# The scan's operand products, the fill's low parts and the scaling of attention's output, from POOL to VectorE

## The chip, the cores and the metric

The kernel runs on one core of a Trainium2 chip. Its time is device microseconds of one execution. TensorE (PE) multiplies matrices; VectorE (DVE), ScalarE (ACT) and GpSimd (POOL) do elementwise work; SyncE (SP) issues most of the DMA transfers. Each engine takes its own queue of instructions in order, and waits on semaphores for what the others have to deliver.

## The reference

One layer of an encoder for 1024 prompt and 256 sample tokens (1280 columns in all), width 1024. Two branches read the same modulated input `h @ w_in`: latent attention with 8 heads, and a recurrence with 8 heads of 64 channels, run once forward and once backward over the tokens. Their outputs are gated, added and projected, and a feed-forward part follows. The part of the recurrence that matters here, for each head and direction:

```python
def step(S, inp):
    r_t, w_t, k_t, v_t, kk_t, a_t = inp
    sa = einsum('bhvk,bhk->bhv', S, -kk_t)
    S = S * w_t + sa[..., :, None] * (kk_t * a_t)[..., None, :] + v_t[..., :, None] * k_t[..., None, :]
    y = einsum('bhvk,bhk->bhv', S, r_t)
    return S, y
```

and beside it `o_mla = softmax(q k) v @ w_mla_o`, and the gates `sigmoid(h @ w_in[gate columns])`.

## The kernel before, in words

Stages follow each other: input products of the recurrence, input products of attention with seven of the sixteen gate tiles, attention, then **the scan with the fill beside it**, then merge, output product, norm and the feed-forward part. Matrix products in the large stages split each factor into a rounded high part and a low part (`hi`, `lo`) and add three products. A weight tile comes by DMA (`wraw`), ScalarE rounds it to `whi`, and another engine subtracts to `wlo` (line 55): POOL unless the caller names VectorE.

The scan (`phase_rwkv`) goes over ten batches of 128 tokens, each in both directions, each in two steps of 64 tokens. For one batch:

- `front` (line 763 on) loads the batch's decay sums, keys and so on, runs a prefix sum on VectorE (`L`, line 774), centres it (line 780), takes exponentials on ScalarE (`E2`, `M`) and multiplies the keys by them into `bk` (line 789: two products 128x512 per direction).
- `left` (line 798 on) makes `lt`: a negated product of `kk` (line 807) and a product of `r` (line 811), four and four of 64x256 per direction and batch.
- `part` multiplies `lt` with `bk` on PE; ScalarE copies the results out, POOL masks them (lines 733 and 738). Of them come the 16 small triangular matrices `aa`.
- `invert` inverts these on VectorE: a transpose `X` (line 856), 31 times a multiply and an addition (lines 865 and 867, the tiles `xt` and `W`), two transposes (869, 871), then two groups of small products on PE (lines 877 and 882, `pw`) with copies between (878, 879, 884, 885).
- `begin` and `step` carry the state `S` through the batch's two steps: products on PE into `py` and `pS`, copied or added by VectorE (`ru` line 917, `xv` line 921, `S` lines 900 and 926) and ScalarE (`yt`, lines 934 and 935). `begin` multiplies two small vectors to `f` (line 895).

The fill (`phase_fill`) is work of other branches that PE does beside the scan: nine gate tiles over three groups of columns (line 1041 the products, line 1154 the tanh), then attention's output: `scaled` loads the unscaled output and the row sums' reciprocals, multiplies them (line 1172), rounds the result on ScalarE (line 1023) and subtracts for the low part (line 1024); `mla_out` multiplies with `w_mla_o` and applies the gate (line 1181). It makes 1368 products of 128x256 or 128x512 on PE. Each gate tile's `whi` and `wlo` are made once, stored, and loaded again for the other two groups of columns. Parts of the merge (`branch`, lines 1063 to 1087) for 512 middle tokens stand near the scan's end too.

The order in each engine's queue is set by a scheduler before the run: it lists the instructions by priority and by a modelled time. The scan's steps have the highest priority (an offset of 4000), the inversions a small one (100), the fill comes after in the program and is put where the model sees room. Tiles have a fixed number of buffers: `ld` (the scan's loads) 5, `bk` 2, `lt` 5 per direction, weights 2, rows of the fill 4, one set for the inversion.

Of the kernel before, what the change touches and what calls it, by code (L numbers as in the profile page):

```python
# [9 lines left out]
ALU = mybir.AluOpType  # L10
# [8 lines left out]
KT = D // P  # L19
# [695 lines left out]
def phase_rwkv(g, ctx):  # L715
# [46 lines left out]
    def front(o, eng):  # L762


        d = o.d

        def cv(ap):
            return ap.rearrange("p (c i) -> p c i", i=64)

        s = load(o, f"s{d}")  # L770
        kq = load(o, f"ka{d}", f"kd{d}"), load(o, f"kd{d}", f"ka{d}")
        kk, r = load(o, "kk"), load(o, "r")
        L, M = half("L"), half("M", 520).rearrange("p (a c i) -> p a c i", a=4, c=2)
        nc.vector.tensor_tensor_scan(L, rst, s, 0.0, ALU.mult, ALU.add)
        f = o.f
        mk = rf.tile([P, 4, 2], F32, tag="mid", name="mid", bufs=2)
        L4 = L.rearrange("p (a c i) -> p a c i", a=4, c=2)
        nc.vector.tensor_scalar(mk, L4[:, :, :, 63], 0.5, None, ALU.mult)
        nc.vector.tensor_scalar(M[:, :, :, 0], mk, -1.0, None, ALU.mult)
        eng.tensor_tensor(M[:, :, :, 1:], L4, mk.unsqueeze(3).broadcast_to([P, 4, 2, 64]), ALU.subtract)  # L780
        E2 = half("E2")
        nc.scalar.activation(E2.rearrange("p (a c i) -> p a c i", a=4, c=2), M[:, :, :, 1:], AF.Exp, scale=-K2)
        nc.scalar.activation(M, M, AF.Exp, scale=K2)
        nc.vector.tensor_tensor(f[:, :, 0:1], mk[:, :, 0:1], mk[:, :, 1:2], ALU.add)
        nc.vector.tensor_copy(f[:, :, 1:3], mk[:, :, ::-1])
        nc.scalar.activation(f, f, AF.Exp, scale=K2)
        bk = rf.tile([P, 8, 2, 64], F32, tag="bk", name="bk", bufs=BK)
        for i in range(2):
            nc.gpsimd.tensor_tensor(bk[:, :, i, :], cv(kq[i]), cv(E2), ALU.mult)
        o.bk, o.kk, o.r, o.L = bk, kk, r, M  # L790

    def values(o):
# [6 lines left out]
    def left(o, st, eng):  # L799
        def pick(ap, rows):  # L800
            return ap[rows].rearrange("p (a c i) -> p a c i", a=4, i=64)[:, :, st, :]
        before, here = o.L[:, :, st, 0:64], o.L[:, :, st, 1:65]
        lt = o.lt[st] = rf.tile([P, 4, 2, P], F32, tag=f"lt{o.d}", name="lt", bufs=LT)
        for e in range(2):
            l = lt[HV[e], :, e, 0:64]
            if eng is nc.vector:
                eng.scalar_tensor_tensor(l, pick(o.kk, HV[e]), -1.0, before[HV[e]], ALU.mult, ALU.mult)
            else:
                eng.tensor_tensor(l, pick(o.kk, HV[e]), before[HV[e]], ALU.mult)
                eng.tensor_scalar(l, l, -1.0, None, ALU.mult)  # L810
            nc.gpsimd.tensor_tensor(lt[HV[e], :, e, 64:128][:, :, ::1 - 2 * o.d], pick(o.r, HV[e]), here[HV[e]], ALU.mult)

    def part(o, st, aa):

# [72 lines left out]
    def begin(bt, sv):  # L887

        if sv.f is None:
            nc.gpsimd.memset(S, 0.0)  # L890
            for e in range(2):
                nc.gpsimd.memset(bt.xv[0][HV[e], :, e, :], 0.0)
        else:
            f = rk.tile([P, 8, 1], F32, tag="fb", name="fb", bufs=2)
            nc.gpsimd.tensor_tensor(f, sv.f, bt.f[:, :, 2:3], ALU.mult)
            place(bt.xv[0], f)

    def place(xv, f):
# [128 lines left out]
def weights(g, src, kt, eng=None):  # L1027
    return [split_w(g, src[:, k0:k0 + 4, :], 4, eng, pool=g.fl, tag=g.ft, rbufs=RB, bufs=WB) for k0 in range(0, kt, 4)]


def product(g, src, kt, parts, ws=None, eng=None):

    ws = ws or weights(g, src, kt, eng)
    for part in parts:
        p = g.fp.tile([P, 512], F32, tag="mm", name="fp")
        c = 0
        for a, n in part:
            for k in range(kt):
                wh, wl = ws[k // 4]
                for i, (ww, aa) in enumerate(((wh, a[0]), (wh, a[1]), (wl, a[0]))):  # L1040
                    g.nc.tensor.matmul(p[:, c:c + n], lhsT=ww[:, k % 4, :], rhs=aa[:, k, :n],  # L1041
                                       start=(k == 0 and i == 0), stop=(k == kt - 1 and i == 2))
            c += n
        yield p[:, :c]
# [73 lines left out]
def phase_fill(g):  # L1118
# [17 lines left out]
    def kept(j, made):  # L1136

        if made is not None:
            for h, w in enumerate(made):
                for e in range(2):  # L1140
                    nc.sync.dma_start(out=g.scr["gw"][j - NB, h, e].bitcast(F32), in_=w[e].bitcast(F32))
            return made
        ws = []
        for h in range(2):
            ws.append([fl.tile([P, 4, P], F32R, tag=g.ft + t, name="w" + t, bufs=WB) for t in ("hi", "lo")])
            for e in range(2):
                nc.sync.dma_start(out=ws[h][e].bitcast(F32), in_=g.scr["gw"][j - NB, h, e].bitcast(F32))
        return ws

    def gate(j, *parts, ws=None):  # L1150
        for p in product(g, io["w_in"][20 + j], KT, [[x[:2] for x in parts]], ws):
            n, c0 = p.shape[-1], parts[0][2]
            t = row("gt", n)
            nc.scalar.activation(t, p, AF.Tanh, scale=0.5)
            nc.sync.dma_start(out=g.scr["gate"][j, :, c0:c0 + n], in_=t)
# [3 lines left out]
    xs = [load(i, c0) for i, c0 in enumerate(spans[0])]  # L1159
    for s in range(3):  # L1160
        for j in js:
            gate(j, *xs, ws=kept(j, weights(g, io["w_in"][20 + j], KT) if s == 0 else None))
        xs = [load(i, c0) for i, c0 in enumerate(spans[s + 1])] if s < 2 else []

    def scaled(a, c0, n):
        for j in range(4):
            raw, bc = row("raw", n), row("bc", n)
            nc.sync.dma_start(out=raw, in_=g.scr["om"][j, :, c0:c0 + n])
            for e in range(2):
                nc.sync.dma_start(out=bc[HV[e]], in_=g.scr["rs"][2 * j + e].rearrange("a t -> (a t)")[c0:c0 + n].unsqueeze(0)  # L1170
                                  .broadcast_to([64, n]))
            nc.gpsimd.tensor_tensor(raw, raw, bc, ALU.mult)
            split_in(g, raw, a[0][:, j, :], a[1][:, j, :])

    def mla_out(*parts):
        for dt in range(KT):
            ts = [row("gt", n) for _, _, n in parts]
            for t, (_, c0, n) in zip(ts, parts):
                nc.sync.dma_start(out=t, in_=g.scr["gate"][dt, :, c0:c0 + n])
            for p, t, (_, c0, n) in zip(product(g, io["w_mla_o"][dt], 4, [[(a, n)] for a, _, n in parts]), ts, parts):  # L1180
                nc.vector.scalar_tensor_tensor(t, t, 1.0, p, ALU.add, ALU.mult)
                nc.sync.dma_start(out=g.scr["xm"][dt, :, c0:c0 + n], in_=t)

# [278 lines left out]
```

## Time and profile before

| | us |
|---|---|
| median of 3 runs (lowest to highest) | 2679.28 (2678.97 to 2682.38) |
| profiled execution | 2674.54 |
| its span | 2672.8 |
| busy in the span: PE / VectorE / ScalarE / POOL | 2498.4 / 1439.4 / 999.9 / 645.9 |
| mean granted TensorE clock | 0.959 of 2.4 GHz |

The span is from the first to the last instruction. Busy time is when an engine works on at least one instruction. PE's busy time comes from modelled ends of pipelined products, so a PE that is busy all the time isn't at its peak. The scan with the fill lies at 885.6 to 1503.3 us of the span, a quarter of it. Stretches are given in microseconds from the span's start.

### The profile page before, as it was taken

The numbers are of one execution on the slowest core, as the hardware profiler recorded it, in microseconds if no ns is written. First come the engines' busy times: TensorE is split into PE (matmuls) and PEld (weight loads), VectorE is DVE, ScalarE is ACT, GpSimd is POOL, SyncE is SP. The second block draws the span as 40 slices with busy tenths as digits, with TensorE's granted clock in tenths as the row PEclk, the third lists the DMA queues.
The fourth block names the chain that finished last, engine by engine and source line by source line (L and its number), as shares of the span: only waits on it lengthen the run. The fifth ranks groups of instructions, "written<-read, shape, count | busy, mean of one in ns | idle before, by whom it ended". The sixth has DMA issues, their size and how long they took to land. (4 is left out here: it accounts for less than half of the span.)

```text
span 2672.8 us, 42383 instructions
## 1 busy us (share of the span) xinstructions
PE 2498.4 (93%) x17018; PEld 2121.9 (79%) x17018; DVE 1439.4 (54%) x2513; ACT 999.9 (37%) x1867; POOL 645.9 (24%) x675
## 2 busy tenths in 40 slices
PE   5999999989998799899997999999999999999997
PEld 3777777778887688888885767788888888888886
DVE  5655652347777678887676587542122222222228
ACT  4422332347676666565552233331110111101114
POOL 2112131021015545443333000132111111111123
PEclk8999999999999688898997999999999999999998
DMA  7654532110003544644655665221111111111113
GB/s 288 230 198 177 211 126 85 47 32 19 18 13 89 173 150 145 196 147 121 191 182 188 203 207 166 89 79 48 40 40 34 38 40 40 40 32 40 40 43 131
DMA packets 188469, 292.36 MB, mean 109 GB/s; under 512 B 16160, under 2 KB 106096, under 8 KB 188272
## 3 DMA queue, kind: packets, MB, share of 16 engines
q1 hardware_dynamic: 174880, 242.07, 28.4%
q0 software_dynamic: 5760, 26.22, 2.4%
q10 hardware_dynamic: 7632, 21.37, 2.3%
q8 instruction: 134, 2.20, 0.3%
q14 instruction: 63, 0.52, 0.1%
HBM read 211.95 MB, written 77.64 MB: 108 GB/s over the span
## 5 line engine op out<-in xcount | busy, mean ns | idle before, releaser
L55 POOL TENSOR_TENSOR wlo<-wraw,whi 128x1024 fp32r<-128x1024 f32 (+2 forms) x149 | 293.9, 1975 | 1343.3 <-ACT whi L53 1129.8
L53 ACT CAST whi<-wraw 128x1024 fp32r<-128x1024 f32 (+2 forms) x212 | 172.6, 819 | 905.3 <-issue 476.1
L67 PE MATMUL mm<-h2h,whi 128*128 128x512 f32 (+1 forms) x1056 | 279.5, 357 | 2.4 <-ACT whi L53 2.4
L67 PE MATMUL mm<-h2h,wlo 128*128 128x512 f32 (+1 forms) x1056 | 279.0, 357 | 1.5 <-POOL wlo L55 1.5
L67 PE MATMUL mm<-h2l,whi 128*128 128x512 f32 (+1 forms) x1056 | 278.5, 356 | 0.0
L67 PE MATMUL mm<-g,whi 128*128 128x512 f32 (+1 forms) x1056 | 240.9, 359 | 6.2 <-DVE ft L1251 5.6
L1041 PE MATMUL fp<-x,whi 128*128 128x256 f32 (+1 forms) x912 | 206.9, 320 | 27.5 <-ACT x L1023 18.4
L67 PEld LDWEIGHTS mm<-g,whi 128*128 128x128 f32 x1056 | 178.0, 190 | 38.0 <-issue 5.7
L67 PEld LDWEIGHTS mm<-h2h,whi 128*128 128x128 f32 x1056 | 177.0, 188 | 33.6 <-ACT whi L53 2.5
L67 PEld LDWEIGHTS mm<-h2h,wlo 128*128 128x128 f32 x1056 | 176.9, 188 | 33.4 <-POOL wlo L55 2.8
L67 PEld LDWEIGHTS mm<-h2l,whi 128*128 128x128 f32 x1056 | 177.1, 188 | 31.2 <-issue 0.5
L1263 DVE SCALAR_TENSOR_TENSOR x<-mm,g2h,x 128x512 f32<-128x512 f32 (+1 forms) x144 | 87.1, 655 | 196.3 <-PE mm L67 196.0
L1041 PEld LDWEIGHTS fp<-x,whi 128*128 128x128 f32 x912 | 156.3, 204 | 39.1 <-ACT x L1023 21.5
L1251 DVE SCALAR_TENSOR_TENSOR ft<-ft,mm 128x512 f32<-128x512 f32 (+1 forms) x66 | 36.1, 594 | 224.2 <-ACT ft L1250 224.1
L67 PE MATMUL mm<-hl,whi 128*128 128x512 f32 (+1 forms) x480 | 147.6, 364 | 7.7 <-DVE hl L265 7.7
L67 PE MATMUL mm<-hh,whi 128*128 128x512 f32 (+1 forms) x480 | 148.0, 366 | 6.4 <-ACT pp L320 3.8
L1041 PE MATMUL fp<-x,wlo 128*128 128x256 f32 (+1 forms) x456 | 146.6, 322 | 6.6 <-POOL wlo L55 3.9
L1252 DVE TENSOR_TENSOR ft<-ft,mm 128x512 f32<-128x512 f32 (+1 forms) x66 | 36.0, 593 | 216.2 <-PE mm L67 216.2
L67 PE MATMUL mm<-hh,wlo 128*128 128x512 f32 (+1 forms) x480 | 145.8, 363 | 0.0
L67 PE MATMUL mm<-g,wlo 128*128 128x512 f32 (+1 forms) x528 | 136.5, 359 | 1.2 <-POOL wlo L55 1.2
L865 DVE TENSOR_TENSOR xt<-W,X 128x126 f32<-128x126 f32 (+22 forms) x310 | 125.8, 406 | 9.0
L867 DVE TENSOR_TENSOR W<-W,xt 128x126 f32<-128x126 f32 (+22 forms) x310 | 120.4, 388 | 8.6
(318 smaller groups left out, 5149.8 us busy)
## 6 DMA issues: line engine op xcount, KB each, us to landing
wraw<-in_w_ffn_in_dram SPq DMA_DIRECT2D x56, 512.0 KB, 3.5
araw<-in_w_ada_dram ACTq DMA_DIRECT2D x32, 512.0 KB, 3.3
wraw<-in_w_ffn_out_dram SPq DMA_DIRECT2D x26, 512.0 KB, 3.6
wraw<-in_w_in_dram SPq DMA_DIRECT2D x20, 512.0 KB, 4.0
x<-scr_h SPq DMA_DIRECT2D x20, 512.0 KB, 7.5
whi<-scr_gw SPq DMA_DIRECT2D x36, 256.0 KB, 3.0
wlo<-scr_gw SPq DMA_DIRECT2D x36, 256.0 KB, 3.5
araw<-in_w_ada_dram SPq DMA_DIRECT2D x16, 512.0 KB, 10.1
```

The lines of the kernel that those rows point to most:

```text
L53: nc.scalar.copy(hi, raw)
L55: (eng or nc.gpsimd).tensor_tensor(lo, raw, hi, ALU.subtract)
L67: nc.tensor.matmul(p[:, :n], lhsT=ww[:, k, :], rhs=aa[:, k, c0:c0 + n], start=(k == 0 and i == 0), stop=(k == kt - 1 and i == 2))
L865: nc.vector.tensor_tensor(tv, W[:, h:, j:j + 1].broadcast_to([P, n, j]), X[:, j:j + 1, 0:j].broadcast_to([P, n, j]), ALU.mult)
L867: nc.vector.tensor_tensor(W[:, h:, 0:j], W[:, h:, 0:j], tv, ALU.add)
L1041: g.nc.tensor.matmul(p[:, c:c + n], lhsT=ww[:, k % 4, :], rhs=aa[:, k, :n], start=(k == 0 and i == 0), stop=(k == kt - 1 and i == 2))
L1251: nc.vector.scalar_tensor_tensor(t[:, :n], t[:, :n], 1.0, u[:, :n], ALU.add, ALU.mult)
L1252: nc.vector.tensor_tensor(t[:, :n], t[:, :n], z[:, :n], ALU.mult)
L1263: nc.vector.scalar_tensor_tensor(x1[:, dt, c0:c0 + n], p[:, :n], g.g2h[:, dt, c0 // TP:c0 // TP + 1], x1[:, dt, c0:c0 + n], ALU.mult, ALU.add)
```

## The change

Seven calls are given to VectorE that were on POOL: the products of `bk` and `lt` in all batches but the first (whose `eng` is POOL, since it is prepared during attention), the product of `f`, the low parts of the fill's weights (gates and `w_mla_o`), and the scaling of attention's output. By the queues 36 of 40 products of `bk`, 72 of 80 of `lt`, all 8 of `f`, 34 low parts and all 12 scalings move.

```diff
--- before.py
+++ after.py
@@ -786,7 +786,7 @@
         nc.scalar.activation(f, f, AF.Exp, scale=K2)
         bk = rf.tile([P, 8, 2, 64], F32, tag="bk", name="bk", bufs=BK)
         for i in range(2):
-            nc.gpsimd.tensor_tensor(bk[:, :, i, :], cv(kq[i]), cv(E2), ALU.mult)
+            eng.tensor_tensor(bk[:, :, i, :], cv(kq[i]), cv(E2), ALU.mult)
         o.bk, o.kk, o.r, o.L = bk, kk, r, M
 
     def values(o):
@@ -808,7 +808,7 @@
             else:
                 eng.tensor_tensor(l, pick(o.kk, HV[e]), before[HV[e]], ALU.mult)
                 eng.tensor_scalar(l, l, -1.0, None, ALU.mult)
-            nc.gpsimd.tensor_tensor(lt[HV[e], :, e, 64:128][:, :, ::1 - 2 * o.d], pick(o.r, HV[e]), here[HV[e]], ALU.mult)
+            eng.tensor_tensor(lt[HV[e], :, e, 64:128][:, :, ::1 - 2 * o.d], pick(o.r, HV[e]), here[HV[e]], ALU.mult)
 
     def part(o, st, aa):
 
@@ -892,7 +892,7 @@
                 nc.gpsimd.memset(bt.xv[0][HV[e], :, e, :], 0.0)
         else:
             f = rk.tile([P, 8, 1], F32, tag="fb", name="fb", bufs=2)
-            nc.gpsimd.tensor_tensor(f, sv.f, bt.f[:, :, 2:3], ALU.mult)
+            nc.vector.tensor_tensor(f, sv.f, bt.f[:, :, 2:3], ALU.mult)
             place(bt.xv[0], f)
 
     def place(xv, f):
@@ -1159,7 +1159,7 @@
     xs = [load(i, c0) for i, c0 in enumerate(spans[0])]
     for s in range(3):
         for j in js:
-            gate(j, *xs, ws=kept(j, weights(g, io["w_in"][20 + j], KT) if s == 0 else None))
+            gate(j, *xs, ws=kept(j, weights(g, io["w_in"][20 + j], KT, nc.vector) if s == 0 else None))
         xs = [load(i, c0) for i, c0 in enumerate(spans[s + 1])] if s < 2 else []
 
     def scaled(a, c0, n):
@@ -1169,7 +1169,7 @@
             for e in range(2):
                 nc.sync.dma_start(out=bc[HV[e]], in_=g.scr["rs"][2 * j + e].rearrange("a t -> (a t)")[c0:c0 + n].unsqueeze(0)
                                   .broadcast_to([64, n]))
-            nc.gpsimd.tensor_tensor(raw, raw, bc, ALU.mult)
+            nc.vector.tensor_tensor(raw, raw, bc, ALU.mult)
             split_in(g, raw, a[0][:, j, :], a[1][:, j, :])
 
     def mla_out(*parts):
@@ -1177,7 +1177,7 @@
             ts = [row("gt", n) for _, _, n in parts]
             for t, (_, c0, n) in zip(ts, parts):
                 nc.sync.dma_start(out=t, in_=g.scr["gate"][dt, :, c0:c0 + n])
-            for p, t, (_, c0, n) in zip(product(g, io["w_mla_o"][dt], 4, [[(a, n)] for a, _, n in parts]), ts, parts):
+            for p, t, (_, c0, n) in zip(product(g, io["w_mla_o"][dt], 4, [[(a, n)] for a, _, n in parts], eng=nc.vector), ts, parts):
                 nc.vector.scalar_tensor_tensor(t, t, 1.0, p, ALU.add, ALU.mult)
                 nc.sync.dma_start(out=g.scr["xm"][dt, :, c0:c0 + n], in_=t)
 
```

The scheduler then orders all queues of this stage anew. Three places show it.

VectorE in the sixth inversion (`xt` and `W` are the inversion's own), before:

```order
L865 TENSOR_TENSOR xt<-W,X 128x126
L867 TENSOR_TENSOR W<-W,xt 128x9x14
L865 TENSOR_TENSOR xt<-W,X 128x130
L867 TENSOR_TENSOR W<-W,xt 128x10x13
L865 TENSOR_TENSOR xt<-W,X 128x120
L867 TENSOR_TENSOR W<-W,xt 128x10x12
L807 SCALAR_TENSOR_TENSOR lt<-ld,M 64x4x64 x2
L917 COPY ru<-py 64x512
L865 TENSOR_TENSOR xt<-W,X 128x121
L867 TENSOR_TENSOR W<-W,xt 128x11x11
L865 TENSOR_TENSOR xt<-W,X 128x110
```

and of the change:

```order
L865 TENSOR_TENSOR xt<-W,X 128x126
L867 TENSOR_TENSOR W<-W,xt 128x9x14
L807 SCALAR_TENSOR_TENSOR lt<-ld,M 64x4x64
L811 TENSOR_TENSOR lt<-ld,M 64x4x64
L807 SCALAR_TENSOR_TENSOR lt<-ld,M 64x4x64
L917 COPY ru<-py 64x512
L811 TENSOR_TENSOR lt<-ld,M 64x4x64
L865 TENSOR_TENSOR xt<-W,X 128x130
L789 TENSOR_TENSOR bk<-ld,E_11399 128x8x64
L867 TENSOR_TENSOR W<-W,xt 128x10x13
L789 TENSOR_TENSOR bk<-ld,E_11399 128x8x64
L865 TENSOR_TENSOR xt<-W,X 128x120
```

The products of `lt` (line 811) and of `bk` (line 789) stand between two steps of the inversion, the former behind the negated product of the same tile, the latter on either side of one step.

VectorE at the end of the eighth inversion, up to the first transpose of the ninth, before:

```order
L865 TENSOR_TENSOR xt<-W,X 128x30
L867 TENSOR_TENSOR W<-W,xt 128x15x2
L865 TENSOR_TENSOR xt<-W,X 128x16
L867 TENSOR_TENSOR W<-W,xt 128x16
L869 STREAM_TRANSPOSE dt<-W 128x32x16
L871 STREAM_TRANSPOSE xr<-dt 128x512
L879 COPY aa<-pw 32x16x32
L856 STREAM_TRANSPOSE X<-aa 128x1024
```

and of the change (`raw` and `x` are attention's output, `gt` its gate):

```order
L867 TENSOR_TENSOR W<-W,xt 128x16
L869 STREAM_TRANSPOSE dt<-W 128x32x16
L1024 TENSOR_TENSOR x<-raw,x 128x256
L871 STREAM_TRANSPOSE xr<-dt 128x512
L1172 TENSOR_TENSOR raw<-raw,bc 128x256 x2
L1024 TENSOR_TENSOR x<-raw,x 128x256 x2
L1181 SCALAR_TENSOR_TENSOR gt<-gt,fp 128x512
L879 COPY aa<-pw 32x16x32
L1181 SCALAR_TENSOR_TENSOR gt<-gt,fp 128x256
L55 TENSOR_TENSOR wlo<-wraw,whi 128x512
L1181 SCALAR_TENSOR_TENSOR gt<-gt,fp 128x512
L856 STREAM_TRANSPOSE X<-aa 128x1024
```

The scaling, the splitting and the gating of attention's output now stand among the last instructions of an inversion, two inversions before the last.

PE from the second half of the scan's last step (`py`, line 931) on, before:

```order
L1041 MATMUL fp<-x,whi 128x512 x2
L1041 MATMUL fp<-x,wlo 128x512
L931 MATMUL py<-xv,arb 64x64 x16
L1041 MATMUL fp<-x,whi 128x256 x2
L1041 MATMUL fp<-x,wlo 128x256
L1041 MATMUL fp<-x,whi 128x256 x2
L1041 MATMUL fp<-x,wlo 128x256
L1041 MATMUL fp<-x,whi 128x256 x2
L1041 MATMUL fp<-x,wlo 128x256
L1041 MATMUL fp<-x,whi 128x256 x2
L1041 MATMUL fp<-x,wlo 128x256
```

and of the change (`or` is the merged output's operand, the next stage's):

```order
L919 MATMUL py<-ru,tt_7623 64x64 x8
L925 MATMUL pS<-xv,bkt 64x64 x8
L931 MATMUL py<-xv,arb 64x64 x8
L913 MATMUL py<-xv,lt 64x64 x32
L919 MATMUL py<-ru,tt_7623 64x64 x16
L931 MATMUL py<-xv,arb 64x64 x16
L1041 MATMUL fp<-or,whi 128x512 x2
L1041 MATMUL fp<-or,wlo 128x512
L1041 MATMUL fp<-or,whi 128x512 x2
L1041 MATMUL fp<-or,wlo 128x512
L1041 MATMUL fp<-or,whi 128x512 x2
```

Before, 20 rows like these last eight, 60 products of the fill, follow the scan's last product; now the next stage's products follow it directly, and 192 instead of 80 of the fill's products stand ahead of the first step.

## Rows read from the trace of the kernel before

**Rows 1.** Busy time by stretch: PE, PEld, VectorE, ScalarE, POOL (count); clock, DMA share, GB/s.

```profile
...
938.60:1000.40 61.80, 58.29 (x685) 53.78 (x686) 47.49 (x98) 35.63 (x79) 31.73 (x43) 0.89 0.50 155
...
1335.90:1379.60 43.70, 42.60 (x619) 39.62 (x620) 32.26 (x80) 29.95 (x68) 14.17 (x26) 1.00 0.54 172
1379.60:1464.40 84.80, 61.85 (x598) 48.89 (x599) 65.07 (x134) 27.14 (x47) 26.32 (x22) 0.83 0.63 194
1464.40:1503.30 38.90, 38.90 (x368) 34.03 (x367) 9.69 (x17) 8.26 (x14) 6.39 (x5) 0.93 0.49 155
...
sum 871.40, PE 786.20 PEld 689.34 DVE 640.69 ACT 422.76 POOL 275.89; mean PE 65.52 PEld 57.44 DVE 53.39 ACT 35.23 POOL 22.99
```

**Rows 2.** Line 856, each inversion's first instruction: ns min/median/max, first and last start.

```profile
L856 DVE STREAM_TRANSPOSE X<-aa x10: 1978/2042/2057, 885.6 to 1379.6; 128x1024 f32<-128x1024 f32 x10
```

**Rows 3.** VectorE's waits, 938.6 to 1379.6: us, times, longest.

```profile
DVE aa L879 <- ACT aa L878: 46.8, 8, 7.5
DVE X L856 <- PE pw L882: 31.2, 9, 5.2
```

**Rows 4.** VectorE in order of time: start, length, instruction.

```profile
1184.77 0.29 DVE L867 TENSOR_TENSOR W<-W,xt 128x126 f32<-128x126 f32 x1
1185.10 1.28 DVE L865 TENSOR_TENSOR xt<-W,X 128x120 f32<-128x120 f32 x1
1186.31 0.67 DVE L926 TENSOR_TENSOR S<-S,pS 128x512 f32<-128x512 f32 x1
1186.90 0.80 DVE L867 TENSOR_TENSOR W<-W,xt 128x120 f32<-128x120 f32 x1
1187.63 0.68 DVE L900 TENSOR_TENSOR S<-S,f 128x512 f32<-128x512 f32 x1
```

**Rows 5.** POOL in the same stretch.

```profile
1184.78 2.78 POOL L789 TENSOR_TENSOR bk<-ld,E 128x512 f32<-128x512 f32 x2 [6.23 <-PE py L931]
```

**Rows 6.** Busy VectorE of the inversion's 62 multiplies and additions, by stretch.

```profile
938.60:1000.40 61.80, 28.45 (x62) 0.89 0.50 155
1335.90:1379.60 43.70, 19.82 (x62) 1.00 0.54 172
```

**Rows 7.** POOL's groups, 885.6 to 1503.3: busy us, mean ns, idle before and releasers.

```profile
L811 POOL TENSOR_TENSOR lt<-ld,M 64x256 f32<-64x256 f32 x68 | 50.2, 738 | 35.2 <-DMA ld<-scr_r 14.4 <-ACT whi L53 12.1 <-DVE W L867 3.0
L789 POOL TENSOR_TENSOR bk<-ld,E 128x512 f32<-128x512 f32 x34 | 45.1, 1340 | 49.1 <-PE py L931 12.5 <-DMA ld<-scr_kd 12.1 <-DMA ld<-scr_ka 10.2
L55 POOL TENSOR_TENSOR wlo<-wraw,whi 128x512 fp32r<-128x512 f32 x33 | 42.2, 1288 | 86.3 <-ACT whi L53 82.9 <-issue 3.1
...
L1172 POOL TENSOR_TENSOR raw<-raw,bc 128x512 f32<-128x512 f32 x8 | 11.4, 1421 | 21.8 <-DMA bc<-scr_rs 16.1 <-DVE xt L865 2.9 <-DVE W L867 2.8
```

**Rows 8.** Line 807, the negated products on VectorE: ns min/median/max.

```profile
L807 DVE SCALAR_TENSOR_TENSOR lt<-ld,M x68: 383/534/2371, 894.7 to 1346.6; 64x256 f32<-64x256 f32 x68
```

**Rows 9.** The chain of waits around the scan's end: start, length, what.

```profile
1502.76 0.59 ACT yt L935
...
1515.48 0.60 DVE wlo L55
```

**Rows 10.** POOL's waits, 938.6 to 1379.6: us, times, longest.

```profile
POOL lt L811 <- DMA ld<-scr_r: 14.4, 5, 4.5
POOL bk L789 <- PE py L931: 12.5, 2, 6.2
POOL bk L789 <- DMA ld<-scr_kd: 12.1, 3, 6.5
POOL bk L789 <- DMA ld<-scr_ka: 10.2, 4, 3.4
```

**Rows 11.** PE's largest group, 1379.6 to 1503.3.

```profile
L1041 PE MATMUL fp<-x,whi 128*128 128x512 f32 (+1 forms) x162 | 51.0, 394 | 20.7 <-ACT x L1023 18.4 <-ACT whi L53 1.2 <-DVE x L1024 1.1
```

**Rows 12.** PE in order of time, from the fill to the next stage.

```profile
1512.42 0.28 PE L1041 MATMUL fp<-x,wlo 128*128 128x256 f32 x1
1513.86 0.73 PE L1041 MATMUL fp<-or,whi 128*128 128x512 f32 x2 [1.16 <-ACT or L1023]
```

## The prediction

> **What bounds the kernel now.** I read the table of stretches first. From 885.6 to 1503.3 us the scan and the fill run side by side, and the windows are cut at the starts of the ten inversions (the reader sees how many, and the first and the last start, in [rows 2]). In [rows 1] the reader is to see that no engine is full there and two are close: over the whole table PE is busy 786 of 871 us, and in the stretch 938.6 to 1000.4 VectorE 47.5 of 61.8 with PE at 58.3. A batch takes 54.9 us on average ((1379.6 - 885.6) / 9 from [rows 2]).
>
> Next the waits of VectorE [rows 3]. Over the eight batches from 938.6 to 1379.6 its two large waits are both inside the inversion: for the copies behind the two small products on PE, 46.8 and 31.2 us, or 9.75 us a batch. The rest of a batch VectorE is at work, with gaps of some 0.04 us between dependent instructions [rows 4]. The inversions stand one behind the other, so a batch lasts as long as VectorE's work in it plus that 9.75. That is the bound of the scan: VectorE's queue, in its order. PE is idle for 3.5 us of the batch from 938.6 [rows 1]: the fill's products take up what the scan leaves.
>
> Then the timeline, VectorE against POOL. [rows 4, 5]: while POOL runs the two products of `bk` (from 1184.78, 2.78 us), an inversion's multiply takes 1.28 us and the next 0.80, where the one before took 0.29. The addition that reads PSUM took 0.67 in the middle of it, as always. POOL's two took 2.78 us there, near twice their mean of 1.34 [rows 7], so they are hardly lengthened. So a part of VectorE's busy time is waiting for POOL. How much, in [rows 6] with the POOL column of [rows 1]: the same 62 instructions took 28.45 us in a batch with 31.73 us of POOL, and 19.82 in one with 14.17. That is 0.49 us of VectorE for 1 us of POOL, for the inversion alone.
>
> **The change part by part.** Everything moved is two-input work of POOL beside the scan [rows 7]: the products of `lt` 50.2 us, of `bk` 45.1, the low parts of the fill 42.2, the scaling 11.4 in eight instructions and, at half of their 1.42 us each, 2.8 in the four of half width: together 152 us. (The eight products of `f`, 128x8, I leave out here and put in below at 1 us in all.)
>
> What goes: 152 x 0.49 = 74 us of stalls in the inversions. The negated products of `lt` on VectorE (68 of them) have a shortest of 0.383 and a median of 0.534 us [rows 8]; 68 x 0.15 = 10 us, of which the moved part of POOL's time (152 of the 276 us in the POOL column's sum) gives some 6. Removed: 80 us.
>
> What comes: by the order 36 products of `bk`, 72 of `lt`, 34 low parts and 12 scalings go to VectorE. VectorE's price of a 128x512 two-input instruction is 0.60 us behind a neighbour [rows 9] to 0.68 alone [rows 4]; of a 64x256 one 0.38 to 0.53 [rows 8], the upper end holding stalls that I expect to go. Low end: 36 x 0.60 + 72 x 0.38 + 34 x 0.60 + 8 x 0.60 + 4 x 0.38 + 1 = 77 us. High end: 24.5 + 38.2 + 23.1 + 5.4 + 2.1 + 1 = 94. I take 80: between two dependent steps of the inversion an independent instruction overlaps its neighbour's end ([rows 4]: 0.67 long, the next starts 0.59 later). So the exchange is even: 0, with ends at -2 and +15, and below, if each us of POOL held VectorE for a whole us, at 77 - 152 = -75.
>
> New waits: VectorE takes its queue in order, and a product that is not ready now holds up the inversion behind it, and the step's copies that PE's next products wait for. On POOL these instructions waited for loads and for the buffer [rows 10]: 14.4 + 12.5 + 12.1 + 10.2 = 49 us in eight batches. POOL came early and had nothing else to do; VectorE comes to them later, since its queue is fuller. Ends: 0 and 49; I take an eighth, +6.
>
> The scaling: POOL took 1.42 us for a 128x512 product [rows 7] and ScalarE, then PE, waited for it; PE's products waited 18.4 us for the rounded `x` in the stretch from 1379.6 [rows 11]. With 0.68 in the place of 1.42, 8 x 0.74 = 6 us of that chain go; I take -5. Ends: -18 and, if the loads behind it set the pace, 0.
>
> The order: PE's queue now ends the fill before the scan ends. Before, 60 of the fill's 1368 products stand behind the last step. The last copy of the scan starts at 1502.76 [rows 9], the fill's last product at 1512.42, and the first of the next stage at 1513.86 [rows 12]: 1513.86 - 1503.35 = 10.5 us. Those products go into PE's idle time from 1379.6 to 1464.4, where PE was busy 61.85 of 84.8 us [rows 1], and what is late next there is the last inversion. Behind the scan the new queue has the next stage's products at once. I take -11. The cost if that cover is gone: the chain of attention's output now stands in the eighth and ninth inversions; [rows 1] show what that mixture does in the tenth, 84.8 us against 54.9. It is not a new cost as long as the tenth gives back what they take.
>
> Sum: 0 + 6 - 5 - 11 = -10 us. The profiled execution took 2674.54 us (span 2672.8), the median of the runs is 4.7 us above it, so 2679.3 - 10 = 2669.
>
> **A rule beside the rows.** On [rows 4, 5]: the Trainium skill, SBUF — State Buffer, section "Who interferes with whom", says that a VectorE instruction with two inputs in SBUF contends with a GpSimd instruction that reads SBUF, and that one with at most one such input does not. The trace agrees: 1.28 against 0.29 us, and 0.67 for the PSUM one. By its exclusive lock for the whole instruction every us of POOL could cost VectorE a us, and the sum would be nearer to the end of -75 than to 0; the measured slope is 0.49.
>
> **The rivals.**
>
> *The waits of the loads move onto VectorE (slower).* Place: VectorE's queue at the products of `bk` and `lt`, in each batch. For it: loads landed just as POOL wanted them [rows 10], and the inversion is the pacer. Against it: VectorE's own two large waits are not for loads [rows 3], and the new queue has inversion steps ahead of each `bk`. Price: two thirds of the 49 us instead of an eighth, +33 for +6, so 2669 + 27 = 2696. It decides from 16 us of such waits: there the gain is gone.
>
> *PE takes the room (no change).* In the batches where the new queue puts more fill ahead of the scan (192 products stand before the first step, 80 before the change) PE has little slack: 58.29 of 61.8 us are busy from 938.6, and 42.60 of 43.7 from 1335.9 [rows 1]. Then the scan ends some 10 us later, and the 11 us behind it only pay for that: 2679. Against it: PE's total work does not change and it has 85 us idle over the table. On the even exchange the Trainium skill speaks too: Perfetto Trace Analysis, section "Optimizing Scalar/DVE Operations", says that since the two engines share a read port, moving work between them might not help; this case's rows agree so far (80 out, 80 in).
>
> *More is given back than the inversions show.* VectorE's other instructions with two SBUF inputs are stalled too. With 0.75 for 0.49, 152 x 0.75 = 114 us go in the inversions' place of 74, which is -40 more and 2629, and PE's 85 us of idle time allow that. For it: a median of 0.534 against a shortest of 0.383 us [rows 8]. Against it: an instruction that reads PSUM, as the 0.67 one in [rows 4], is not stalled, and each step of the scan has three of that kind (`ru`, `xv`, the addition to `S`). The lock rule above would put the time here.
>
> **How the numbers follow.** The forecast 2669, with a range of its own from 2658 to 2676: 0.42. Waits on VectorE: 0.28. PE takes the room: 0.20. More given back: 0.10. A difference of about 0.2%, 5 us, is what a measurement can tell, so faster is below 2674, slower above 2684.6. Faster: 0.36 of the forecast's 0.42, all of the third rival, 0.01 of PE's: 0.47. Same: 0.06 and 0.15: 0.21. Slower: 0.28 and 0.04: 0.32. The range of 8 in 10 leaves out half of the third rival and a part of the first one's far end: 2642 to 2700.
>
> **What would show it.** Right: in the changed kernel's profile the inversion's 62 instructions take 20 us or less in a batch, with POOL at some 12 us a batch ((276 - 152) / 10); VectorE's busy time from the first inversion to the scan's end stays within 15 us; a batch in the middle lasts 53 to 56 us; the first product of the next stage follows the scan's last within 2 us. By the order the eighth inversion gets 36 instructions of the fill's chain and the ninth 17, at 0.6 us each some 20 and 10 us; the tenth loses 21 and the wait of 18.4 us, so it shrinks by about as much as these two grow; the last stretch of 38.9 us shrinks, since PE has none of the fill left there. Wrong: VectorE waiting for loads of `kd`, `ka` or `r`, or for the exponential, over 16 us in sum; a batch over 58 us; or the scan ending later than before by more than 11 us.

## The result, and the profile after

The changed kernel took 2656.45 us (median of 6 runs, 2648.19 to 2660.46) beside 2676.98 us of the kernel before (median of 6, 2666.06 to 2682.38): a ratio of 0.9925 [0.9907, 0.9943], 20.5 us less. The forecast was 2669, the range 2642 to 2700. The measured gain is thus twice the forecast one; the time lies inside the wide range and just outside the forecast's own, 2658 to 2676. The profiled execution of the changed kernel took 2652.19 us (span 2650.5), 22 less than that of before. Runs of one kernel differ by up to 0.9% here, so a trace shows where time went in one execution, and the ratios say whether it counts.

The stretches of the kernel after, cut at its ten inversions and at the scan's end (columns as in [rows 1]):

```profile
888.10:945.20 57.10, 52.38 (x507) 47.23 (x506) 42.23 (x111) 36.49 (x84) 14.41 (x27) 0.94 0.73 230
945.20:1004.80 59.60, 59.17 (x741) 55.53 (x741) 46.28 (x116) 37.74 (x81) 11.86 (x21) 1.00 0.61 197
...
1173.30:1226.10 52.80, 48.87 (x657) 45.42 (x657) 41.05 (x108) 32.59 (x74) 10.59 (x21) 0.97 0.61 188
1226.10:1286.90 60.80, 52.10 (x653) 45.94 (x654) 47.44 (x119) 36.02 (x80) 10.57 (x21) 0.92 0.65 194
1286.90:1361.10 74.20, 65.11 (x649) 53.60 (x649) 59.21 (x144) 40.40 (x86) 11.09 (x21) 0.86 0.61 183
1361.10:1418.80 57.70, 57.38 (x677) 50.90 (x678) 47.00 (x111) 32.59 (x70) 10.58 (x21) 1.00 0.53 163
1418.80:1474.20 55.40, 32.08 (x461) 30.10 (x459) 42.13 (x111) 16.80 (x28) 0.00 (x0) 0.67 0.26 78
1474.20:1493.60 19.40, 17.26 (x256) 16.53 (x255) 4.13 (x7) 5.25 (x9) 0.00 (x0) 0.88 0.06 15
sum 605.50, PE 541.73 PEld 490.46 DVE 452.45 ACT 334.74 POOL 100.51; mean PE 49.25 PEld 44.59 DVE 41.13 ACT 30.43 POOL 9.14
```

and the scan of the kernel before in one window:

```profile
885.60:1503.30 617.70, 550.73 (x6544) 499.39 (x6544) 459.87 (x978) 332.38 (x719) 254.02 (x352) 0.89 0.53 163
```

The reader is to see three things. VectorE has 166 instructions more (155 moved ones, 11 of the fill's and the next stage's that the new order brings in) and is busy 7.4 us less, while POOL's time falls from 254.0 to 100.5 us. The first nine batches are longer than before, 530.7 us ((1418.8 - 888.1)) against 494.0 by [rows 2]; the eighth (54.4 to 74.2) and the ninth (43.7 to 57.7) are 33.8 of these 36.7 us. And what follows the last inversion is shorter: 74.8 us (55.4 + 19.4) against 123.7 (84.8 + 38.9 in [rows 1]). So the scan itself gains 12 us in this trace and the stages behind it 12.7 (1169.5 to 1156.8); the scan began 2.5 us later. A second trace of the same kernel (e11 below) has VectorE busy for the same 452.4 us, but a scan of 612.0: of the scan's gain 6 to 12 us are shown, no exact size.

The inversion's 62 multiplies and additions in two batches after (VectorE busy, clock, DMA; before, [rows 6]):

```profile
945.20:1004.80 59.60, 18.33 (x62) 1.00 0.61 197
...
1418.80:1474.20 55.40, 15.67 (x62) 0.67 0.26 78
```

VectorE's groups in the scan, first before:

```profile
L865 DVE TENSOR_TENSOR xt<-W,X 128x126 f32<-128x126 f32 (+22 forms) x310 | 125.8, 406 | 9.0
L867 DVE TENSOR_TENSOR W<-W,xt 128x126 f32<-128x126 f32 (+22 forms) x310 | 120.4, 388 | 8.6
L807 DVE SCALAR_TENSOR_TENSOR lt<-ld,M 64x256 f32<-64x256 f32 x68 | 40.7, 598 | 2.3 <-DMA ld<-scr_kk 1.3
```

then after, with the moved work (two of the 36 low parts of line 55 are the next stage's):

```profile
L867 DVE TENSOR_TENSOR W<-W,xt 128x126 f32<-128x126 f32 (+22 forms) x310 | 89.3, 288 | 7.8
L865 DVE TENSOR_TENSOR xt<-W,X 128x126 f32<-128x126 f32 (+22 forms) x310 | 89.3, 288 | 7.8
...
L807 DVE SCALAR_TENSOR_TENSOR lt<-ld,M 64x256 f32<-64x256 f32 x68 | 30.8, 453 | 3.7 <-DMA ld<-scr_kk 2.6
L811 DVE TENSOR_TENSOR lt<-ld,M 64x256 f32<-64x256 f32 x68 | 30.8, 453 | 4.0 <-DMA ld<-scr_r 3.6
L55 DVE TENSOR_TENSOR wlo<-wraw,whi 128x512 fp32r<-128x512 f32 x36 | 25.1, 702 | 8.7 <-ACT whi L53 8.2
L789 DVE TENSOR_TENSOR bk<-ld,E 128x512 f32<-128x512 f32 x34 | 23.7, 711 | 8.5 <-DMA ld<-scr_ka 4.8 <-PE pT L833 2.3 <-ACT E L782 0.8
L1172 DVE TENSOR_TENSOR raw<-raw,bc 128x512 f32<-128x512 f32 (+1 forms) x12 | 7.6, 632 | 10.3 <-DMA bc<-scr_rs 10.3
```

Stalls given back: 125.8 + 120.4 - 89.3 - 89.3 = 67.6 us in the inversions, 9.9 in the negated products. Work added: 30.8 + 25.1 x 34/36 + 23.7 + 7.6 + 1 (for `f`) = 86.8 us of the instructions' own lengths; part of each lies over a neighbour's end.

VectorE's waits after, 945.2 to 1418.8 (before, [rows 3]):

```profile
DVE aa L879 <- ACT aa L878: 27.3, 6, 8.2
DVE X L856 <- PE pw L882: 23.3, 8, 5.2
DVE raw L1172 <- DMA bc<-scr_rs: 10.3, 8, 2.9
DVE L L774 <- DMA ld<-scr_s: 9.1, 8, 2.2
...
DVE bk L789 <- DMA ld<-scr_ka: 4.0, 6, 0.8
DVE lt L811 <- DMA ld<-scr_r: 3.3, 5, 0.9
...
DVE x L1024 <- ACT x L1023: 1.7, 2, 1.1
```

The wait for the inversion's copies fell from 46.8 to 27.3 us, since independent work now stands in it; waits of the moved instructions come in its place.

PE after, in order of time, at the scan's end (before, [rows 12]):

```profile
1490.91 2.11 PE L931 MATMUL py<-xv,arb 64*64 64x64 f32 x32
1492.95 0.72 PE L1041 MATMUL fp<-or,whi 128*128 128x512 f32 x2
```

The next stage starts on PE with no gap, 0.7 us ahead of the scan's end (1493.64, the end of its last copy) where it stood 10.5 us behind it before: 11.2 us earlier.

### The profile page after: what moved, and what is told of

It is laid out like the page before. It is cut to its first block, busy times and chain, and to the rows that moved or that the text cites. A ratio compares the mean times of both kernels' runs of the same rounds, so it can differ in the third digit from the quotient of the medians.

```text
span 2650.5 us, 42268 instructions
## 1 busy us (share of the span) xinstructions
PE 2482.6 (94%) x17018; PEld 2106.5 (79%) x17018; DVE 1428.0 (54%) x2675; ACT 998.2 (38%) x1867; POOL 488.2 (18%) x513
## 4 chain that ended last, share of the span: by engine, by line
PE 76%; DVE 11%; DMA 7%; ACT 2%; issue 2%; SPq 0%; POOL 0%; DVEq 0%; ACTq 0%; POOLq 0%
PE mm L67 45%; PE fp L1041 7%; PE s L627 3%; PE py L913 2%; PE o L661 2%; PE proj L560 2%; PE gps L453 2%; PE t L648 2%; PE pA L820 2%; PE pS L925 1%; PE py L931 1%; DMA ld<-scr_s 1%; PE py L919 1%; PE ada_ps L170 1%; PE lora L369 1%
## 5 line engine op out<-in xcount | busy, mean ns | idle before, releaser
L55 POOL TENSOR_TENSOR wlo<-wraw,whi 128x1024 fp32r<-128x1024 f32 (+3 forms) x115 | 251.1, 2185 | 1334.6 <-ACT whi L53 1332.7
L67 PEld LDWEIGHTS mm<-h2h,whi 128*128 128x128 f32 x1056 | 177.2, 188 | 33.8 <-ACT whi L53 2.6
L67 PEld LDWEIGHTS mm<-h2l,whi 128*128 128x128 f32 x1056 | 177.2, 188 | 31.2 <-issue 0.5
L1041 PEld LDWEIGHTS fp<-x,whi 128*128 128x128 f32 x912 | 150.9, 197 | 32.0 <-ACT x L1023 14.9
L627 PE MATMUL s<-kb,q 128*128 128x512 f32 (+1 forms) x432 | 112.0, 392 | 2.3 <-ACT pr L633 2.2
L650 DVE TENSOR_TENSOR pt<-t,pt 128x512 fp32r<-128x512 f32 x144 | 92.6, 654 | 27.1 <-ACT pt L649 26.8
```

Source lines behind the costliest of these rows:

```text
L55: (eng or nc.gpsimd).tensor_tensor(lo, raw, hi, ALU.subtract)
L67: nc.tensor.matmul(p[:, :n], lhsT=ww[:, k, :], rhs=aa[:, k, c0:c0 + n], start=(k == 0 and i == 0), stop=(k == kt - 1 and i == 2))
L627: nc.tensor.matmul(s[:, o:o + w], lhsT=a[:, tt * P:(tt + 1) * P], rhs=b[:, c0 + o:c0 + o + w], start=(m == 0), stop=(m == 2))
L650: nc.vector.tensor_tensor(lo[:, :w4, us], t[:, :w4, :], hi[:, :w4, us], ALU.subtract)
```

## The experiments

Each kernel was timed in 5 rounds beside the kernel before, in three groups on three chips; the median of before was 2676.47 us beside e1 to e4, 2680.03 beside e5 to e8 and 2681.41 beside e9 to e11. So the ratios compare, the medians only within a group. "Rest" is the span from the scan's end on; "inversions" is VectorE's busy time in the 620 multiplies and additions. Times are from the runs, the other columns from one trace each, in us (those of e1 and e9 are of the shortest of seven runs, 13 and 19 us below the median); "idle" is the scan less VectorE's busy time.

| kernel | median | ratio to before | scan | VectorE busy, idle | inversions | POOL | rest |
|---|---|---|---|---|---|---|---|
| before | | 1 | 617.7 | 459.9, 157.8 | 246.1 | 254.0 | 1169.5 |
| after | 2656.45 | 0.9925 [0.9907, 0.9943] | 605.5 | 452.4, 153.1 | 178.7 | 100.5 | 1156.8 |
| e1 | 2694.97 | 1.0052 [1.0033, 1.0071] | 635.1 | 452.2, 182.9 | 228.2 | 255.5 | 1160.4 |
| e2 | 2705.62 | 1.0102 [1.0084, 1.0121] | 646.8 | 446.4, 200.4 | 177.0 | 103.3 | 1170.0 |
| e3 | 2715.28 | 1.0139 [1.0120, 1.0157] | 665.2 | 522.5, 142.7 | 222.3 | 227.5 | 1159.1 |
| e4 | 2663.89 | 0.9947 [0.9930, 0.9964] | 619.7 | 454.9, 164.8 | 177.2 | 215.9 | 1160.0 |
| e5 | 2663.71 | 0.9940 [0.9921, 0.9959] | 617.3 | 453.6, 163.7 | 198.4 | 160.3 | 1156.9 |
| e6 | 2656.22 | 0.9911 [0.9887, 0.9934] | 608.3 | 464.5, 143.8 | 222.6 | 202.7 | 1162.7 |
| e7 | 2667.12 | 0.9943 [0.9920, 0.9965] | 614.6 | 449.3, 165.3 | 179.8 | 115.7 | 1159.5 |
| e8 | 2668.04 | 0.9958 [0.9942, 0.9973] | 616.4 | 452.1, 164.3 | 177.9 | 104.3 | 1159.7 |
| e9 | 2665.44 | 0.9933 [0.9908, 0.9958] | 599.0 | 455.1, 143.9 | 197.8 | 156.2 | 1160.4 |
| e10 | 2654.87 | 0.9900 [0.9878, 0.9921] | 603.1 | 466.0, 137.1 | 206.8 | 150.9 | 1159.5 |
| e11 | 2664.92 | 0.9946 [0.9927, 0.9966] | 612.0 | 452.4, 159.6 | 177.1 | 100.6 | 1157.7 |

### Order and engines apart (e1, e2)

e1 is the kernel before, all the moved calls on POOL (the diff has six, not seven), with the queues of PE, VectorE, ScalarE and SyncE held to the changed kernel's order by edges that set the order and wait for nothing; POOL's own queue is left to the scheduler:

```diff
+    for code in ORDER.values():          # one list of instructions for each engine, from the changed kernel
+        ...
+        for a, b in zip(mine, mine[1:]):
+            tc.add_manual_dep(b, a.name, mybir.DependencyInfo(mybir.DependencyClass.NoSync, mybir.DependencyReason.DATA),
+                              reason="order")
```

> The engines of the kernel before (all seven calls on POOL), but the queues of PE, VectorE, ScalarE and SP in the order of the changed kernel (the moved instructions left out of VectorE's). My theory, two halves: VectorE is stalled by POOL as before (some 80 us of stalls) and freed of some 80 us of work, so the scan itself gains nothing, and the fill still ends before the scan: the order's 11 us remain, 2666 us. Rival 'order alone': all of the gain is the order, 2656. Rival 'readiness': the products arrive later from POOL than this order wants them, so it is slower than before, over 2680.

It was slower: 1.0052 [1.0033, 1.0071], 14 us by the ratio and 18.5 by the medians. The forecast of 2666 failed; the rival "readiness" (over 2680) came true. The new order alone gains nothing. Its scan in one window, and VectorE's waits from 948.1 to 1444.0 (the same nine starts as above):

```profile
884.40:1519.50 635.10, 553.99 (x6604) 500.11 (x6603) 452.22 (x989) 335.20 (x725) 255.53 (x353) 0.91 0.53 163
```

```profile
DVE aa L879 <- ACT aa L878: 37.5, 7, 8.5
...
DVE x L1024 <- ACT x L1023: 14.3, 10, 3.6
DVE gt L1181 <- PE fp L1041: 8.7, 5, 3.2
```

This is the cleanest pair of the study. In the same order VectorE is busy 452.22 us with the work on POOL and 452.45 us with the work on itself: 155 instructions more cost it nothing. The 30 us between the two scans (23 with e11's trace) are all idle time of VectorE. With POOL in the chain the rounded `x` comes late (14.3 us against 1.7), the gates wait for its products (8.7 against 3.2), and the inversion's waits have less to fill them (37.5 against 27.3).

e2 is the reverse: the changed kernel's engines, with PE, ScalarE, SyncE and VectorE's former instructions held to the order of before; the moved ones stand where the scheduler then puts them.

> The engines of the changed kernel, but every instruction that is not moved in the order of the kernel before, on PE, VectorE, ScalarE and SP. My theory: the stalls go, the work comes, the fill still ends after the scan: the scan's 10 us remain and the order's 11 are lost, 2666 us. Rival 'order alone': no gain, 2677. Rival 'readiness': products are ready sooner in an order that doesn't ask for it, 2670 to 2677.

It was slower still, 1.0102 [1.0084, 1.0121], outside the forecast of 2666 and both rivals. The inversions are as fast as in the changed kernel (177.0 us), and yet VectorE is idle 200 us. Its waits from 942.2 to 1398.3:

```profile
DVE aa L879 <- ACT aa L878: 42.5, 8, 10.5
...
DVE lt L811 <- DMA ld<-scr_r: 11.6, 7, 3.3
DVE wlo L55 <- ACT whi L53: 10.0, 5, 2.8
DVE bk L789 <- PE pT L833: 6.4, 3, 5.4
DVE bk L789 <- DMA ld<-scr_ka: 5.1, 4, 1.6
```

The moved instructions wait here for their loads, for ScalarE's rounding and for PE, and the inversion's waits stay unfilled. The waits for `r`, `ka`, `kd` and the exponential are 11.6 + 5.1 + 1.8 + 1.7 = 20.2 us, over the prediction's mark of 16: this is the rival "the waits of the loads move onto VectorE", in an order in which it comes true. The fill ends behind the scan as before (its last product at 1543.60, the scan's last copy at 1533.93):

```profile
1543.60 0.28 PE L1041 MATMUL fp<-x,wlo 128*128 128x256 f32 x1
1544.99 0.73 PE L1041 MATMUL fp<-or,whi 128*128 128x512 f32 x2 [1.11 <-ACT or L1023]
```

and the rest is 1170.0 us, like before's 1169.5 and unlike the 1156.8 of the changed kernel. In the changed kernel's order (e1, e3, e4, e11) it is 1157.7 to 1160.4, whatever the engines. The fill's end is thus worth 9 to 13 us to the rest, and it is the order that sets it. e4 also shows that holding an order costs little in itself: its ratio, 0.9947, is that of the changed kernel in e11, 0.9946.

### What a us of POOL costs (e3, e4)

e3 is the changed kernel in its own order with 160 products more on POOL, whose result nothing uses; each reads two inputs (a constant) behind one of the masks:

```diff
+        tc.keep_in_program_order(nc.gpsimd.tensor_tensor(du[:, 0:256], rst[:, 0:256], rst[:, 256:512], ALU.mult))
```

> The changed kernel, queues of PE, VectorE, ScalarE and SP in its own order, with 160 two-input products of 128x256 bf16 on POOL behind its masks, whose result nobody uses: by the price of POOL's 64x256 products some 0.7 us each, 110 us of POOL in all. My theory: each us of POOL reading two tiles costs the inversion 0.49 us, so the inversion's 62 instructions go from 18 back to some 23 us a batch, and the kernel is 30 to 55 us slower than the changed one, 2686 to 2711. Rivals 'order alone' and 'readiness': POOL's being busy costs nothing, within 5 us of 2656.

1.0139 [1.0120, 1.0157]: 52 to 57 us more than the changed kernel by the ratios (of e11 and of the first measurement), just over the upper end of what was expected. POOL is busy 127 us more, VectorE 70 us more in the same instructions (522.5 - 452.4), 43.7 of them in the inversions: 0.55 and 0.34 us for each us of POOL. The timeline of VectorE and POOL in that kernel (its lines stand three further down: 868 and 870 are 865 and 867):

```profile
1153.91 3.90 POOL L742 TENSOR_TENSOR du<-rst 128x256 bf16<-128x256 bf16 x5
1154.02 0.88 DVE L814 TENSOR_TENSOR lt<-ld,M 64x256 f32<-64x256 f32 x1
...
1156.55 0.57 DVE L870 TENSOR_TENSOR W<-W,xt 128x56 f32<-128x56 f32 x1
1157.16 0.74 DVE L868 TENSOR_TENSOR xt<-W,X 128x81 f32<-128x81 f32 x1
1157.94 0.24 DVE L870 TENSOR_TENSOR W<-W,xt 128x81 f32<-128x81 f32 x1
```

e4 has two fills of a constant in the place of each product, which read nothing:

```diff
+        tc.keep_in_program_order(nc.gpsimd.memset(du, 0.0))
+        tc.keep_in_program_order(nc.gpsimd.memset(du, 0.0))
```

> As the run with POOL's products, but with two memsets of 128x320 bf16 in the place of each, some 0.36 us each, so about the same busy time on POOL, with nothing read. My theory, with the stall due to reads: within 5 us of the changed kernel, 2656, and 18 us of the inversion's instructions a batch. Rival 'any work of POOL stalls': as slow as the run with products.

0.9947 [0.9930, 0.9964]: by the ratio it can't be told from the changed kernel, though POOL is busy 115 us more. The inversions stay at 177.2 us. In its timeline (lines four further down) the steps beside a fill are short, and the one beside a mask, which reads one input, is not:

```profile
1184.40 0.41 POOL L740 TENSOR_SCALAR_AFFINE_SELECT arb<-arb 64x256 f32<-64x256 f32 x1
1184.46 0.44 DVE L869 TENSOR_TENSOR xt<-W,X 128x78 f32<-128x78 f32 x1
1184.76 0.36 POOL L742 MEMSET du<- 128x320 bf16 x1
1184.93 0.24 DVE L871 TENSOR_TENSOR W<-W,xt 128x78 f32<-128x78 f32 x1
1185.18 0.36 POOL L743 MEMSET du<- 128x320 bf16 x1
1185.20 0.26 DVE L869 TENSOR_TENSOR xt<-W,X 128x100 f32<-128x100 f32 x1
```

These are single steps; added up over each trace, the 620 steps of the inversions say the same. Against the shortest step of the same kind and shape, the 137 of e4 that lay beside fills alone took 0.01 us more, as did the 339 beside nothing; 70 beside masks alone took 0.16 more, and in e3 the 78 beside products alone 0.37. So it is POOL's reading that holds VectorE up, not POOL's being at work.

### The parts of the change, each with the order that the scheduler then makes (e5, e6, e7, e9, e10, e11)

e5 moves the scan's products alone (`bk`, `lt`, `f`), e6 the fill's part alone (low parts and scaling):

```diff
-            gate(j, *xs, ws=kept(j, weights(g, io["w_in"][20 + j], KT, nc.vector) if s == 0 else None))   # e5
+            gate(j, *xs, ws=kept(j, weights(g, io["w_in"][20 + j], KT) if s == 0 else None))
-            eng.tensor_tensor(bk[:, :, i, :], cv(kq[i]), cv(E2), ALU.mult)                               # e6
+            nc.gpsimd.tensor_tensor(bk[:, :, i, :], cv(kq[i]), cv(E2), ALU.mult)
...
```

> Only the products of bk, lt and f go to VectorE; the fill's low parts and the scaling stay on POOL; the scheduler orders anew. By its queue the fill ends with the last step (1368 of 1368 products) and gives PE something to do in the last two batches. My theory: POOL keeps 57 us of the 152 us beside the scan, so some 28 us of stalls stay, and some 30 us of work stay off VectorE; the exchange is even, the order's 11 us are there: 2655 to 2665. Rival 'order alone': as the changed kernel or better, since the end is filled better, 2645 to 2656. Rival 'the parts only act together': 2670 or more.

> Only the fill's low parts and the scaling go to VectorE; bk, lt and f stay on POOL; the scheduler orders anew, and by its queue the fill ends with the last step here too. My theory: two thirds of the stalls stay (some 50 us of 80), a third of the work comes; even exchange and the order's 11 us, 2660 to 2670. Rival 'order alone': 2650 to 2660. Rival 'the parts only act together': 2672 or more.

Both gain nearly what the whole gains: 0.9940 [0.9921, 0.9959] and 0.9911 [0.9887, 0.9934]; e5 came as forecast, e6 below its forecast and inside the range of "order alone". The gains don't add, and they don't follow the inversions' stalls: e6 has 222.6 us of inversions, 44 more than the changed kernel, and is no slower. In both the first product of the next stage stands at the scan's end (0.7 us ahead of it in the trace), and the rest is 1156.9 and 1162.7 us against 1169.5. In e5's trace that is all of the gain; its scan, 617.3 us, is as long as before's.

e7 is the changed kernel with the scaling back on POOL (line 1172).

> The changed kernel with the scaling of attention's output back on POOL, ordered anew; all else as in the changed kernel. My theory: 14 us of POOL's reads come back (7 us of stalls), 7 us of work go from VectorE, and the chain to PE is 0.74 us longer twelve times, hidden in part: 2656 to 2664. Rival, the waits for the loads of the scaling cost VectorE more than the stalls (10.3 us in the changed kernel's trace): 2646 to 2654.

0.9943 [0.9920, 0.9965], which overlaps the change's own interval: inconclusive (its median of 2667.12 lies outside both ranges that were named). PE's wait for the rounded `x` is read over the whole scan, since in the changed kernel the first of them, 6.0 us, ends at 1274.3, in the seventh batch. After, e7, e1 and e2, in this order (before 18.4, all of it in [rows 11]):

```profile
L1041 PE MATMUL fp<-x,whi 128*128 128x256 f32 (+1 forms) x912 | 202.0, 314 | 18.6 <-ACT x L1023 13.0
L1041 PE MATMUL fp<-x,whi 128*128 128x256 f32 (+1 forms) x912 | 201.6, 314 | 23.0 <-ACT x L1023 15.4
L1041 PE MATMUL fp<-x,whi 128*128 128x256 f32 (+1 forms) x912 | 206.0, 319 | 22.3 <-ACT x L1023 15.3
L1041 PE MATMUL fp<-x,whi 128*128 128x256 f32 (+1 forms) x912 | 209.5, 323 | 27.3 <-ACT x L1023 12.0
```

With the scaling on VectorE the wait is 13.0 us in the new order and 12.0 in the old one (e2); with it on POOL 15.4 (e7) and 15.3 (e1) in the new one and 18.4 in the old one. So by one trace each the engine takes 2.3 to 6.4 us off it (in e1 and e2 the other moved work changes engines with it), the order at most 3.1.

e9 and e10 move the fill's part and one half of the scan's: e9 `bk`, e10 `lt` (each leaves the other, and `f`, on POOL). e11 is the changed kernel once more, on the same chip.

> The fill's low parts and scaling and the products of bk on VectorE; lt and f stay on POOL; ordered anew, and the fill ends before the scan's last step. By what was measured the exchange of stalls for work is even for any part, and the 11 us behind the scan are there: 2650 to 2662. Rival: each further part moved to VectorE adds waits in its queue, so between the fill part alone and the whole, or a little above, 2655 to 2668.

> The fill's low parts and scaling and the products of lt on VectorE; bk and f stay on POOL; ordered anew, and the fill ends with the scan's last steps. Theory and rival as for the run with bk: 2650 to 2662, or 2655 to 2668. If lt's short products, 0.4 us on VectorE against 0.7 on POOL, are the better ones to move, it is the faster of the two.

> The changed kernel itself, once more, beside these two on the same chip: 2656 within 6 us. What differs by less from it isn't told apart.

e10 took 2654.87 us (2645.95 to 2657.94), e11 2664.92, before 2681.41 there. e10's interval, [0.9878, 0.9921], lies wholly below that of e11, [0.9927, 0.9966]: on that chip it beats both kernels, by about 10 us and 27. It does overlap the change's first interval, [0.9907, 0.9943], taken at another time. e11 was expected within 6 us of 2656 and missed that by 3: one kernel gave 0.9925 and 0.9946, so ratios that lie 0.2% apart in different groups are not told apart. e10's scan differs from the changed kernel's in two places: the eighth batch is 53.7 us long (by the starts of its inversions, 1273.5 and 1327.2), and the tail still has fill. Its window from the last inversion to the scan's end:

```profile
1390.50:1486.40 95.90, 86.50 (x899) 76.57 (x899) 62.40 (x149) 29.52 (x51) 0.00 (x0) 0.87 0.51 156
```

PE is busy 86.5 of 95.9 us behind the last inversion, where the changed kernel has 49.3 (32.08 + 17.26) of 74.8, at a clock of 0.67 for most of it. e6's trace and e9's have the same two marks (an eighth batch of 52.2 and 54.9 us, and 85.3 of 96.3 and 86.3 of 95.5 us of PE behind the last inversion). e9's scan is the shortest, 599.0 us, but its profiled execution, 2646.45 us, is the lowest of its seven; by the ratio it can't be told from the change, and its median lies outside its forecast and inside the rival's range. That these two marks make e10's gain is a reading of these traces; no run moved them alone.

### The inversion first (e8)

To take the fill's chain out of the eighth inversion, its priority was raised:

```diff
-LT, LDB, EB, YB, BK, HP, HI, IB, TT = 5, 5, 4, 1, 2, 4000, 100, 1, 2
+LT, LDB, EB, YB, BK, HP, HI, IB, TT = 5, 5, 4, 1, 2, 4000, 300, 1, 2
```

> The changed kernel with the inversions' priority offset 300 in the place of 100, so that the fill's instructions on VectorE give way to them; engines as in the changed kernel. The fill's queue on PE differs little (1289 of 1368 products before the 17th step instead of 1320). My theory, in which stalls and work set the time: within 6 us of 2656. Rival 'order alone', with the place of the fill's chain in the eighth and ninth inversions deciding: at least 10 us away from it, either way.

A miss: 0.9958 [0.9942, 0.9973], no better than the change. Its median is 12 us above 2656, as the rival had it, but 3 above e11's, so neither is decided. The eighth batch is still 77.7 us, with VectorE busy 57.91 of it. About as many instructions of VectorE stand in it (143 and 144); an offset of 300 doesn't take the fill's chain out.

## Why the prediction was right, step by step

**The exchange of stalls and work.** Forecast: 80 us out, 80 in, with VectorE's busy time within 15 us. Measured: 7.4 us less, or 0.2 in one order (e1 against after). This is shown. Its parts: 67.6 us of inversion stalls for the 74 forecast (0.44 us for one of POOL, not 0.49), 9.9 for the 6 of the negated products, and 86.8 of work for the 80. The slope depends on the order too: from e1 to after, in one order, 49.5 us (228.2 - 178.7) went for 155 of POOL, 0.32. That the moved work costs so little is in part that it overlaps: the lengths of all VectorE's instructions in the scan add up to 489.1 us where the engine was busy 452.4, before to 483.2 for 459.9 (added up over each trace).

**New waits.** Forecast: 6 us for `bk` and `lt`, with 16 as the mark of the rival. The waits for `ka`, `r`, the exponential and `kd` come to 4.0 + 3.3 + 0.8 + 0.3 = 8.4 us. The rival did not come true here; e2, with 20.2, shows that it does where the order doesn't suit. Two waits that the sum didn't name are larger: the scaling's for its load (10.3) and the prefix sum's for `s` (9.1, before 1.5). They are paid by the 19.5 us less at the inversion's copies.

**The scaling.** Forecast -5, between -18 and 0. PE's wait for the rounded `x` fell by 5.4 us over the scan (18.4 to 13.0). The size was right, and the reason in part: e1, e2 and e7 put 2.3 to 6.4 us on the engine. That the chain had been moved two batches forward was not in this term.

**The end of the fill.** Forecast -11. Measured 11.2 us at the scan's end, and 9 to 13 in the rest (before and e2 against the kernels in the changed order). The reason is shown.

**Where the batches stand.** The eighth and ninth grew by 19.8 and 14.0 us (forecast 20 and 10), the tenth and the last stretch shrank by 29.4 and 19.5. A middle batch of 53 to 56 us held for the fourth to the sixth alone (54.9, 54.4, 52.8); the second, third and seventh took 59.6, 59.2 and 60.8. A batch over 58 us had been named as a sign of being wrong, and there were four; but before had three (61.8, 58.3 and 84.8), so the sign could tell little. In the second PE was busy 59.17 of 59.60 us with 741 products, 685 before, and in the ninth 57.38 of 57.70, where the batch grew by 14.0: there PE did take the room, as that rival said, but the tail gave more back.

**The size.** The forecast was 10 us, the trace has 22 and the medians 20.5. The mis-sized term is the scan's own: the sum of exchange, waits and scaling was forecast at +1, and it measured -12 (617.7 to 605.5), in e11's trace -6. Some 7.4 of it are VectorE's busy time, in both traces; its idle time fell by 4.7 in the one and rose by 1.8 in the other, so no change of it is shown. The sum took the order as given but for the fill's end. That the time still lay in the range of 8 in 10 owes as much to its width as to the sum. e1 and e2 show that order and engines are worth something only together: from before, the engines alone cost 29 us of scan and the order alone 17, both at once gain 6 to 12 (e2 is one way to place the moved instructions in the old order, not the best one). TensorE's granted clock in the scan differs as well, 0.89 before, 0.92 after, 0.91 in e1 and 0.86 in e2. What it adds was not separated; a higher clock alone does not make the gain, since e1 has one and is 17 us longer. Why the scheduler's order suits one assignment so well and e10's still better was not settled; e5, e6, e7 and e9 lie within a few tenths of a per cent, in other orders each.

The chip's part is told by the runs e3 and e4. In the two timelines above a VectorE step with two inputs takes 0.57 and 0.74 us beside POOL's products and 0.24 to 0.26 beside a fill. The Trainium skill, SBUF — State Buffer, section "Who interferes with whom", says that a VectorE instruction with two inputs in SBUF contends with a GpSimd instruction that reads SBUF, and not with one that only writes it; both traces agree. By its exclusive lock for a whole instruction a us of POOL could cost VectorE up to one; the runs have 0.55 of busy time, which does not decide on the lock, since VectorE is not at such instructions all the time.

## What to carry to other kernels

Here an engine that was stalled by another's reads took over that work at no cost in busy time (452.2 and 452.5 us); find the slope by adding reads to the one that is to be relieved, before moving anything. Then look at the queues, not at the sums: the moved instruction pays where it fills a wait of the new engine, and costs where its input isn't there yet. Try the parts of such a change apart and in pairs, since each makes the scheduler lay all queues anew.

## What was not expected of the hardware

POOL's reading costs VectorE 0.55 us of busy time per us, and POOL's filling with a constant nothing that could be measured (2.4 us for 115). POOL itself is held up less, but not never: of e3's 160 products the shortest took 0.66 us and the middle one 0.68, the five above 0.78 each (3.90 / 5), 21 over 1 us and the longest 1.69. And TensorE's granted clock stood at 0.67, so mostly at the lower of its two levels (1.2 and 2.4 GHz), in the tenth batch after, where PE was busy 32.08 of 55.4 us; in e10, with fill left, it was 0.87 from the last inversion to the scan's end.
